# A decoder block on one Trainium2 core: the relative-position bias scratch written through a 128-partition copy, and 64 bytes of padding ahead of the weight buffers

## The chip, the core and the metric

The kernel runs on one core of a Trainium2 chip. The metric is device time in microseconds (us) of one execution. A profile is one further execution, recorded by the hardware profiler. PE is TensorE's matmul, PEld its weight load, DVE is VectorE, ACT ScalarE, POOL GpSimd, SP SyncE, which here issues the weight transfers.

## The reference

One layer for 256 tokens of width 2048, all in float32. Only what matters here is shown:

```
x = x + 0.5 * swiglu(rms_norm(x, g1), w1_gate, w1_up, w1_down)          # d_ff = 5632
z = rms_norm(x, gm) @ w_in                    # q, k, v, glu_a, glu_b, gate_a, gate_c
bias = rel_bias_table[t5_bucket(max(qpos - kpos, 0))]                   # 8 heads, 32 buckets
s = q @ k.T / 8 + bias, and -1e30 where kpos > qpos                     # two softmaxes per head
o = (softmax(s1) - lam * softmax(s2)) @ v
u = conv31(glu_a * sigmoid(glu_b)); layer norm; silu
x = x + (sigmoid(gate_a) * (o @ w_attn) + sigmoid(gate_c) * (u @ w_conv)) @ w_out
x = x + 0.5 * swiglu(rms_norm(x, g2), w2_gate, w2_up, w2_down)
out = rms_norm(x, final_g)
```

The bias depends on qpos - kpos alone, so each head's 256 x 256 bias is made of one row of 384 values, shifted by one place for each query.

## The kernel before, in words

**The matmuls.** Every product is float32 made of float32r parts. `Weights` (lines 42 to 102) streams all weights in units of 1 MB: four k-tiles by 512 columns, 8 KB in each of 128 partitions. SP issues one transfer for each unit (line 58) into one of three raw buffers `w`. `split_to` (line 76) takes half a unit at a time: ACT copies the rounded high part into `wh` (line 87), DVE subtracts to get the low part `wl` (line 88). There are four `wh` and four `wl` buffers of 4 KB per partition. A raw buffer's next transfer is issued once both of its halves are split.

Two helpers multiply. `lin` (line 292) holds a weight slice of 128 columns as the stationary operand and moves the activations: for each k-tile a "high" matmul over 512 columns (`wh`; line 305) and a "low" one over 256 columns (`wl`; line 310). One such pair is the step of all up, gate, q, k, GLU and output products, and of the first FFN's down product: 4288 pairs in all. `lin_tok` (line 341, through `tok_products`, lines 333 to 339) holds activations as the stationary operand and moves 512 columns of `wl` (line 337) or `wh` (lines 338 and 339): v, the two gates, the attention and convolution branches, and the second FFN's down product. In its very last stage (lines 880 to 894 and 902 to 915) four halves of the weights are split into `qh` and `ql`, which lie in the activations' region Q, in place of `wh` and `wl`.

**Side work.** `Side` (line 110) interleaves small jobs with the matmuls. `tick` is called once for a k-tile pair and column tile; a job of rate 0.1 takes one step in ten ticks, some 7 us of matmuls. The order of every engine's queue is thus fixed when the program is built, and an instruction on POOL that waits for nothing runs as soon as those ahead of it on POOL are done.

**The bias.** `bias_rows` (line 463) is such a job. POOL fills `bias_row` (8 partitions, one for each head, 384 values), then issues one DMA for each head (line 477) that reads that head's single partition 128 times and writes 128 rows of 384 values into the DRAM scratch `row_d` (rows 385 values apart). `bias_load` (line 652) later reads `row_d` with a row step of 384, which shifts each query's row by one. Between the job's steps POOL's queue has the gate products `s_t` of `ffn_up` (line 369), each of which waits for ACT.

**Where the tiles lie.** Tiles are laid out one after another in each partition. `xT`, the regions P and Q (two tiles of 16 KB each: activations as `h`, `a`, `hm`, `mg`, and `qh`, `ql`) and `s_t`/`y_sb` begin at multiples of 1 KB. `u_sb` (line 517) comes next, 8 x 286 values, that is 9152 bytes, or 8 x 1024 + 960. All that follows begins 960 bytes past a multiple of 1 KB: the two `sga`/`sgc` tiles of 16 KB, the three `w`, the four `wh`, the four `wl` and most work tiles.

Of the kernel before, what the change touches and what calls it, by code (L numbers as in the profile page):

```python
# [9 lines left out]
F32 = mybir.dt.float32  # L10
# [5 lines left out]
P = 128  # L16
T = 256
D = 2048
FF = 5632
H = 8  # L20
# [11 lines left out]
def bucket(n):  # L32
    if n < 16:
        return n
    return min(31, 16 + int(math.log(n / 16) / math.log(8) * 16))
# [98 lines left out]
def block_kernel(  # L134
# [5 lines left out]
    nc = tc.nc  # L140

    const = ctx.enter_context(tc.tile_pool(name="const", bufs=1))
    big = ctx.enter_context(tc.tile_pool(name="big", bufs=1))
# [3 lines left out]
    dram = ctx.enter_context(tc.tile_pool(name="dram", bufs=1, space=bass.MemoryType.DRAM))  # L147
# [310 lines left out]

    row_d = dram.tile([H, P, 385], F32, name="row_d")

    def bias_rows():
        row = work.tile([H, 384], F32, name="bias_row", tag="s2", bufs=1)

        nc.gpsimd.memset(row[:, 256:384], NEG)
        rel = 0
        while rel < 256:
            end = rel
            while end < 256 and bucket(end) == bucket(rel):  # L470
                end += 1
            b = bucket(rel)
            nc.gpsimd.tensor_copy(row[:, 256 - end:256 - rel], loads["tab"][:, b:b + 1].broadcast_to([H, end - rel]))
            rel = end
            yield
        for h in range(H):
            nc.gpsimd.dma_start(out=row_d[h:h + 1, :, 0:384], in_=row[h:h + 1].unsqueeze(1).broadcast_to([1, P, 384]))
            yield


    side.add(bias_rows(), 0.1, delay=256)


# [30 lines left out]

    neglam = small.tile([P, 1], F32, name="neglam", bufs=1)
    U0 = KW - 1
    u_sb = big.tile([P, 8, U0 + T], F32, name="u_sb")
    y_sb = big.tile([P, 8, T], F32, name="y_sb", tag="y")

    def mixer_setup():  # L520
# [462 lines left out]
```

## Time and profile before

| | |
|---|---|
| median of 3 runs | 2148.82 us (2148.69 to 2148.85) |
| profiled execution, its own time | 2143.47 us |
| its span, first to last instruction | 2141.7 us |
| mean granted TensorE clock over the span | 0.994 of 2.4 GHz |
| moved by DMA | 395.95 MB, of it 390.10 MB by the queue of SP |

The span is split into engines' busy time in the rows below. A window row gives, for a stretch, each engine's busy time and in brackets how many instructions were running in it, the granted clock as a share of 2.4 GHz, the mean busy share of the 16 DMA engines and what they moved. A timeline row is an instruction's start, its duration, engine, line and operands, and in square brackets the idle time of the engine just before it with what ended that. Matmuls overlap, so the step from one start to the next, not the duration, is what a matmul costs.

### The profile page before, as it was taken

Reading aid. Unit: us, or ns where it says so; the run is one execution under the profiler, and the core shown is the slowest. Engines: PE = TensorE matmul, PEld = TensorE weight load, DVE = VectorE, ACT = ScalarE, POOL = GpSimd, SP = SyncE. Lnnn points to the kernel's source line nnn. Section 1 sums busy time; section 2 is a strip of 40 time slices with the busy share of each in tenths; the row PEclk is TensorE's granted clock in tenths of the full one; section 3 lists DMA queues with packets and bytes.
Section 4 is the critical chain, followed back from the end, with each engine's and each line's share of the span. In section 5 each row is a group of like instructions: output and inputs, shape, how many; then the busy total and the mean of one; then the engine's idle time right before and its main releaser. Section 6 shows DMA issues by size and latency. Waiting matters only on the chain. (4 is left out here: it accounts for less than half of the span.)

```text
span 2141.7 us, 28362 instructions
## 1 busy us (share of the span) xinstructions
PE 2104.0 (98%) x11230; PEld 1790.3 (84%) x11230; DVE 1389.4 (65%) x1915; ACT 1027.7 (48%) x1456; POOL 189.0 (9%) x226
## 2 busy tenths in 40 slices
PE   8999999979999999999999999999999999999998
PEld 6888888867888888888778788888888888888887
DVE  8666556635556776789888766665654656545665
ACT  5544344433345555455555744554543444434444
POOL 6101011110011110000000000200100001000011
PEclk9999999989999999999999999999999999999999
DMA  6655555786555555555554555555555555555553
GB/s 236 203 196 180 194 186 189 192 115 214 183 192 179 186 190 197 181 180 178 182 168 169 190 183 177 177 201 192 178 197 180 180 194 193 180 193 177 197 183 132
DMA packets 57446, 395.95 MB, mean 185 GB/s; under 512 B 6864, under 2 KB 6896, under 8 KB 10464
## 3 DMA queue, kind: packets, MB, share of 16 engines
q1 hardware_dynamic: 55872, 390.10, 52.3%
q0 software_dynamic: 1440, 4.03, 2.6%
q8 instruction: 88, 1.44, 0.3%
q14 instruction: 46, 0.38, 0.0%
HBM read 390.43 MB, written 3.67 MB: 184 GB/s over the span
## 5 line engine op out<-in xcount | busy, mean ns | idle before, releaser
L88 DVE TENSOR_TENSOR wl<-w,wh 128x1024 fp32r<-128x1024 f32 x731 | 902.7, 1248 | 607.8 <-ACT wh L87 600.6
L87 ACT ACTIVATE wh<-w 128x1024 fp32r<-128x1024 f32 x731 | 764.8, 1057 | 821.2 <-PE ps_mm L305 546.5
L305 PE MATMUL ps_mm<-h,wh 128*128 128x512 f32 x2816 | 981.7, 396 | 5.9 <-DVE h L229 5.7
L310 PE MATMUL ps_mm<-h,wl 128*128 128x256 f32 x2816 | 762.4, 281 | 3.5 <-DVE wl L88 3.3
L305 PEld LDWEIGHTS ps_mm<-h,wh 128*128 128x128 f32 x2816 | 518.7, 188 | 115.0 <-ACT wh L71 5.7
L310 PEld LDWEIGHTS ps_mm<-h,wl 128*128 128x128 f32 x2816 | 528.1, 188 | 22.3 <-DVE wl L88 5.7
L305 PE MATMUL ps_mm<-a,wh 128*128 128x512 f32 x704 | 246.0, 397 | 18.1 <-ACT wh L87 18.1
L369 POOL TENSOR_TENSOR s_t<-s_t,rstd 128x256 f32<-128x256 f32 x88 | 85.7, 974 | 1201.2 <-ACT s_t L368 1201.2
L310 PE MATMUL ps_mm<-a,wl 128*128 128x256 f32 x704 | 190.9, 282 | 0.5 <-DVE wl L88 0.5
L305 PE MATMUL ps_mm<-hm,wh 128*128 128x512 f32 x512 | 178.9, 396 | 0.0
L305 PEld LDWEIGHTS ps_mm<-a,wh 128*128 128x128 f32 x704 | 130.2, 189 | 45.5 <-ACT wh L87 18.4
L310 PE MATMUL ps_mm<-hm,wl 128*128 128x256 f32 x512 | 138.4, 281 | 0.0
L310 PEld LDWEIGHTS ps_mm<-a,wl 128*128 128x128 f32 x704 | 133.0, 189 | 5.5 <-DVE wl L88 1.0
L337 PE MATMUL ps_mm<-wl,a 128*128 128x512 f32 (+1 forms) x344 | 133.9, 389 | 0.0
L338 PE MATMUL ps_mm<-wh,a 128*128 128x512 f32 (+1 forms) x344 | 133.8, 389 | 0.0
L339 PE MATMUL ps_mm<-wh,a 128*128 128x512 f32 (+1 forms) x344 | 133.8, 389 | 0.0
L337 PE MATMUL ps_mm<-wl,hm 128*128 128x512 f32 x320 | 130.6, 408 | 0.0
L339 PE MATMUL ps_mm<-wh,hm 128*128 128x512 f32 x320 | 126.5, 395 | 0.0
L338 PE MATMUL ps_mm<-wh,hm 128*128 128x512 f32 x320 | 126.4, 395 | 0.0
L305 PEld LDWEIGHTS ps_mm<-hm,wh 128*128 128x128 f32 x512 | 94.4, 188 | 20.4 <-issue 0.7
L571 DVE SCALAR_TENSOR_TENSOR y_sb<-u_sb,cw_sb,y_sb 128x256 f32<-128x256 f32 x240 | 105.3, 478 | 0.0
L354 ACT ACTIVATE rh<-ps_mm 128x256 f32<-128x256 f32 x208 | 77.5, 373 | 45.8 <-PE ps_mm L305 45.7
(192 smaller groups left out, 1808.9 us busy)
## 6 DMA issues: line engine op xcount, KB each, us to landing
w<-in_ffn_w_up_dram SPq DMA_DIRECT2D x88, 1024.0 KB, 4.9
w<-in_ffn_w_down_dram SPq DMA_DIRECT2D x88, 1024.0 KB, 4.8
w<-in_ffn_w_gate_dram SPq DMA_DIRECT2D x85, 1024.0 KB, 4.9
w<-in_w_in_dram SPq DMA_DIRECT2D x72, 1024.0 KB, 4.8
w<-in_w_out_dram SPq DMA_DIRECT2D x16, 1024.0 KB, 4.9
w<-in_w_attn_branch_dram SPq DMA_DIRECT2D x8, 1024.0 KB, 4.8
w<-in_w_conv_branch_dram SPq DMA_DIRECT2D x8, 1024.0 KB, 4.8
w<-in_ffn_w_gate_dram SPq DMA_DIRECT2D x5, 512.0 KB, 8.9
```

The lines of the kernel that those rows point to most:

```text
L87: self.nc.scalar.activation(wh, w, AF.Copy)
L88: self.nc.vector.tensor_tensor(wl, w, wh.bitcast(F32), ALU.subtract)
L305: nc.tensor.matmul(ps[ct], lhsT=w, rhs=xs(kt), start=(kt == 0), stop=(kt == nk - 1))
L310: nc.tensor.matmul(ps[ct][:, T:2 * T], lhsT=w, rhs=xs(kt)[:, 0:T], start=False, stop=False)
L337: nc.tensor.matmul(ps, lhsT=hi, rhs=wl[:, kk, :], start=(first and kk == 0), stop=False)
L338: nc.tensor.matmul(ps, lhsT=hi, rhs=wh[:, kk, :], start=False, stop=False)
L339: nc.tensor.matmul(ps, lhsT=lo, rhs=wh[:, kk, :], start=False, stop=(last and kk == KH - 1))
L354: nc.scalar.activation(r, ps[:, T:2 * T], AF.Copy, scale=scale)
L369: nc.gpsimd.tensor_tensor(s, s, rstd, ALU.mult)
L571: nc.vector.scalar_tensor_tensor(y, src, w, y, ALU.mult, ALU.add)
```

## The change

Two parts. The first replaces the eight DMAs of `bias_rows` by nine: POOL stores `row` once to a DRAM scratch `row_1` (12 KB); four DMAs, two heads each, read it back, the same 3 KB for each of 128 partitions, into a tile `spread` of 12 KB per partition in the region `sga`; four DMAs, two heads each, write `spread` to `row_d`. The scratch `row_d` gets the same values at the same places. The job has one step more. The second part makes `u_sb` 16 values longer, with the same view of it as before, so that all tiles behind it move up by 64 bytes and begin at a multiple of 1 KB.

```
+    row_1 = dram.tile([H, 384], F32, name="row_1")
     row_d = dram.tile([H, P, 385], F32, name="row_d")
 
     def bias_rows():
...
-        for h in range(H):
-            nc.gpsimd.dma_start(out=row_d[h:h + 1, :, 0:384], in_=row[h:h + 1].unsqueeze(1).broadcast_to([1, P, 384]))
+        nc.gpsimd.dma_start(out=row_1, in_=row)
+        yield
+        spread = big.tile([P, H, 384], F32, name="spread", tag="sga")
+        for h in range(0, H, 2):
+            nc.gpsimd.dma_start(out=spread[:, h:h + 2], in_=bass.AP(tensor=row_1.tensor, offset=row_1.offset + h * 384,
+                                                                  ap=[[0, P], [1, 2 * 384]]))
+            yield
+        for h in range(0, H, 2):
+            nc.gpsimd.dma_start(out=row_d[h:h + 2, :, 0:384].rearrange("h p c -> p h c"), in_=spread[:, h:h + 2])
             yield
...
-    u_sb = big.tile([P, 8, U0 + T], F32, name="u_sb")
+
+    u_sb = big.tile([P, 8 * (U0 + T) + 16], F32, name="u_sb")
+    u_sb = u_sb[:, 0:8 * (U0 + T)].rearrange("p (c t) -> p c t", c=8)
     y_sb = big.tile([P, 8, T], F32, name="y_sb", tag="y")
```

## Rows read from the trace of the kernel before

**Rows 1.** The page's first part: busy time, share of span, instructions.

```profile
PE 2104.0 (98%) x11230; PEld 1790.3 (84%) x11230; DVE 1389.4 (65%) x1915; ACT 1027.7 (48%) x1456; POOL 189.0 (9%) x226
```

**Rows 2.** Windows of 20 us; the first line names the columns.

```profile
core 0: us, PE busy (x) PEld busy (x) DVE busy (x) ACT busy (x) POOL busy (x), PEclk, DMA share, GB/s
...
460.00:480.00 20.00, 7.63 (x44) 6.42 (x42) 3.22 (x8) 1.61 (x5) 0.00 (x0) 0.76 0.93 68
480.00:500.00 20.00, 13.82 (x66) 11.67 (x67) 8.98 (x9) 7.73 (x9) 0.00 (x0) 0.73 0.73 264
...
980.00:1000.00 20.00, 20.00 (x98) 15.90 (x97) 19.41 (x41) 11.96 (x26) 0.00 (x0) 1.00 0.54 181
```

**Rows 3.** Timeline of PE around its one long gap.

```profile
467.35 0.28 PE L310 MATMUL ps_mm<-a,wl 128*128 128x256 f32 x1
485.71 0.79 PE L305 MATMUL ps_mm<-a,wh 128*128 128x512 f32 x1 [18.08 <-ACT wh L87]
...
495.15 0.39 PE L305 MATMUL ps_mm<-a,wh 128*128 128x512 f32 x1
```

**Rows 4.** Waits: engine and line, waited for, us in total, times, longest.

```profile
ACT wh L87 <- DMA w<-in_ffn_w_down_dram: 25.3, 4, 20.9
```

**Rows 5.** Timeline of POOL, its DMA issues and the instruction after them.

```profile
403.30 1.09 POOL L477 DMA_DIRECT2D row_d<-bias_row  x2 [0.30 <-POOL bias_row L473]
...
439.90 0.55 POOL L477 DMA_DIRECT2D row_d<-bias_row  x1
...
444.95 2.60 POOL L477 DMA_DIRECT2D row_d<-bias_row  x5
593.83 0.74 POOL L369 TENSOR_TENSOR s_t<-s_t,rstd 128x256 f32<-128x256 f32 x1 [146.28 <-ACT s_t L368]
```

**Rows 6.** The tile bias_row: issue to landing of its eight DMAs.

```profile
DMA to landing us min/median/max: 9.6/17.2/36.2
```

**Rows 7.** A window of 4 us while those DMAs are in flight.

```profile
456.00:460.00 4.00, 4.00 (x25) 3.46 (x23) 1.98 (x3) 1.90 (x4) 0.00 (x0) 1.00 0.95 27
```

**Rows 8.** Timeline of PE in the last stage, moving operand wl/wh, then ql/qh.

```profile
2104.80 0.39 PE L339 MATMUL ps_mm<-wh,a 128*128 128x512 f32 x1
...
2111.10 0.39 PE L339 MATMUL ps_mm<-wh,a 128*128 128x512 f32 x1
...
2112.72 0.39 PE L337 MATMUL ps_mm<-ql,a 128*128 128x512 f32 x1
...
2116.57 0.39 PE L339 MATMUL ps_mm<-qh,a 128*128 128x512 f32 x1
```

**Rows 9.** Groups of PE by form, line 337: 512-column matmuls on wl.

```profile
L337 PE MATMUL ps_mm<-wl,hm 128*128 128x512 f32 x320 | 130.6, 408 | 0.0
...
L337 PE MATMUL ps_mm<-wl,a 128*128 128x512 f32 x328 | 129.4, 395 | 0.0
...
L337 PE MATMUL ps_mm<-wl,cT 128*128 128x512 f32 x64 | 25.8, 403 | 0.0
L337 PE MATMUL ps_mm<-wl,oT 128*128 128x512 f32 x64 | 25.3, 396 | 0.0
```

**Rows 10.** Timeline of PE in lin, first and last of two runs of pairs.

```profile
105.10 0.39 PE L305 MATMUL ps_mm<-h,wh 128*128 128x512 f32 x1
...
107.89 0.39 PE L305 MATMUL ps_mm<-h,wh 128*128 128x512 f32 x1
...
599.93 0.39 PE L305 MATMUL ps_mm<-h,wh 128*128 128x512 f32 x1
...
607.70 0.40 PE L305 MATMUL ps_mm<-h,wh 128*128 128x512 f32 x1
```

**Rows 11.** DMA issues: count, KB each, median us to landing.

```profile
out_dram<-x SPq DMA_DIRECT2D x8, 256.0 KB, 2.7
...
row_d<-bias_row POOLq DMA_DIRECT2D x8, 192.0 KB, 17.2
...
fg<-in_final_norm_g_dram POOLq DMA_DIRECT2D x1, 1024.0 KB, 6.8
```

## The prediction

> **What bounds the kernel now.** I began with the page's first part: PE is busy 98% of the span, DVE 65%, ACT 48% [rows 1]. So TensorE sets the time nearly everywhere, and only two things can change it: a stretch in which PE stands still, or what one matmul costs.
>
> Windows of 20 us show PE at 20.00 in nearly every one from 40 to 2120 us; the two far below it lie together, from 460 to 500 [rows 2]. There PE works 7.63 and 13.82 us, the granted clock falls to 0.76 and 0.73 on average, and the DMA engines are 0.93 busy while they move only 68 GB/s. Another window, from 980, has a share of 0.54 and 181 GB/s. The reader should see an engine set that is occupied without moving bytes.
>
> The timeline puts the gap between 467.35 and 485.71 us: PE idles 18.08 us for ACT's split of `wh` [rows 3], and ACT had itself waited 20.9 us for a transfer of down weights [rows 4]. POOL's timeline gives the reason: two bias DMAs went out at 403.30, one at 439.90 and five back to back from 444.95, because nothing else stood in POOL's queue [rows 5]. The slowest landed 36.2 us after its issue [rows 6]. Five DMAs of 196,608 bytes in 36.2 us are 27.2 GB/s; a window amid them shows 27 GB/s for all queues together at a share of 0.95 [rows 7]. All 16 engines hold packets of the one source partition, and SP's weights sit behind them until PE's stock is used up.
>
> The cost of one matmul is read where nothing else disturbs it, in the last stage. On `wh`/`wl`, 27 steps run from 2104.80 to 2111.10: 233.3 ns each. On `qh`/`ql`, 17 steps run from 2112.72 to 2116.57: 226.5 ns [rows 8]. Line, shape and stationary tile are the same, PE never waits; only the place of the moving operand differs, 960 bytes past a multiple of 1 KB against 0.
>
> **The change, part by part.** *The stall.* From 467.35 to 495.15 PE started 39 matmuls, 19 pairs and one low, in 27.80 us [rows 3]. At the rate before the stall, 8 pairs in 2.79 us, or 348.8 ns each [rows 10], they need 19 x 0.349 + 0.12 = 6.75 us (the low taken as a third of a pair). The stall thus costs **21.05 us**: the 18.1 us gap, and some 3 us in which PE, after standing still, ran at the lower of its two levels, 1.2 GHz (the first high matmul lasts 0.79 us, the last one quoted 0.39), until the clock rose again.
>
> Is it gone? The nine new DMAs keep POOL's places: `row_1` and the first read-back near 403, the second at 440, then two read-backs and four writes from 445 on. POOL now waits for landings: the first read-back for `row_1`, each write for its read-back. Behind these waits stands only the next `s_t`, at 593.83, which now follows 146.28 us of idleness [rows 5]; nobody waits for POOL before that. The ninth issue costs another 0.5 us there (2.60 us for five). The read-back's nearest row is `fg`, the same 8 KB to 128 partitions, 1 MB in 6.8 us; so 384 KB take at most about that. The write's nearest row is `out`, 256 KB from 128 partitions in 2.7 us, so 384 KB take 4.1 us; the other end is the old DMA's 27.2 GB/s, 14.5 us [rows 6, 11]. I take 4.1, since source layout and not DRAM is what `out` and the new write share. The 36.2 us hold made a gap of 18.1 us, so PE's stock covers 18 us. The burst is 2 x 0.39 + 4 x 0.39 = 2.36 MB; at the 264 GB/s of the recovering window [rows 2] that is 9 us. It fits twice, so I count the whole 21.05 us. If the cover fails, weights are late again at the same place.
>
> *The pad.* It moves all behind `u_sb` from 960 to 0 modulo 1024. The moving operands on line 337 outside region Q are 320 + 328 + 64 + 64 = 776 matmuls of 512 columns [rows 9], and lines 338 and 339 have as many: 2328. At 233.3 - 226.5 = 6.8 ns each that is **15.8 us**. Ends: 0, if something other than alignment separates the two places, and 15.8. I take 15.8, because the pair of rows differs in little else. The one stage where a faster PE may meet another engine is around 980 to 1000, DVE at 19.41 of 20 us [rows 2]; it is short, and I leave its tenths of a us to the range.
>
> [...]
>
> *lin.* Its 512- and 256-column moving operands lie in P and Q, already at multiples of 1 KB; only the stationary slices move. Its pairs run at two rates, 348.8 ns and, 22 pairs from 599.93 to 607.70, 353.2 ns [rows 10], on the same code and the same buffers. So I take **0**. The ends: were each half of a pair to gain as the rows of the last stage do (2.9%), 10 ns on 4288 pairs, 44 us. The other way, all pairs at one of the two rates against all at the other differ by 4288 x 4.4 ns = 19 us; a program laid out anew may fall either way, so 8 us up or down for the range.
>
> *Costed at nothing:* the ACT and DVE splits and the weight transfers start at other addresses, but PE hides them (DVE 65%, ACT 48%); `spread` takes `sga`, whose next user is written only in the mixer; one further step of the job delays nothing that is due.
>
> **Sum.** 2143.47 - 21.05 - 15.8 = 2106.6 for the profiled execution, which stands 5.35 us (0.25%) below the median of the runs. Against the median: 2148.82 - 36.85 = **2112.0 us**.
>
> **Rivals.** (a) *The pad does nothing.* For it: the two places differ in address as well as alignment, and lin's two rates show that steps can differ for other reasons. Against: inside the last stage the rate changes exactly with the operand. 2148.82 - 21.05 = **2127.8**. [...]
>
> (b) *lin gains as well*, by its stationary slices: 2112 - 44 = **2068**. For: lin's high matmul has an aligned moving operand and still does not step at 226.5. Against: its two rates at equal addresses, which alignment cannot explain.
>
> (c) *The slow side was the DRAM write*, rows of 1536 bytes at a step of 1540, not the single source partition. Then the last burst grows from 5 x 0.197 to 4 x 0.393 = 1.57 MB, at 27.2 GB/s 57.8 us; the hold is 21.6 us longer and so is the gap. With the pad's gain 2148.82 + 21.6 - 15.8 = **2154.6**, slower. It decides once the burst holds the weights over 52 us, where what the stall gains in length outweighs the pad. For: the rows are the same as before. Against: `out` writes at 97 GB/s including its latency [rows 11].
>
> (d) *A remnant of the stall*: four writes of 4.1 us in a row and two reads make 19 us or more, just past the cover. A gap of a few us and a spell at the lower clock: 2116 to 2124.
>
> **How the numbers follow.** Forecast 0.55, (a) 0.22, (b) 0.12, (c) 0.05, (d) 0.06. The time is the forecast's. The range goes from 2097 (the forecast with lin at its quicker rate, and part of (b)'s gain) to 2133 (rival (a), with some of lin's loss); it leaves out most of (b) and all of (c). A measurement of this kernel tells about 0.2% (4 us) from no change. All cases but (c) lie more than that below 2148.8; I keep 0.03 of them back for mishaps that cancel. So faster 0.92, same 0.03, slower 0.05.
>
> **What would show it.** Right: no gap of PE near 467, windows 460 to 500 at 20.00 with the clock at 1.00; read-backs and writes of 384 KB landing within 10 us; steps of 226 to 227 ns on lines 337 to 339 throughout, also on `wl` and `wh` in the last stage, equal to those on `ql`. Wrong on the pad: 233 ns stays there. Wrong on lin: pairs near 340 ns. Wrong on the write: landings over 14 us and ACT again waiting for down weights. DVE ending waits of PE between 960 and 1200 would mean that the pad's gain was spent there.

## The result and the profile after

The changed kernel takes 2117.49 us, median of 4 runs (2115.86 to 2119.97), against 2148.84 us of the kernel before in the same comparison (4 runs, 2148.69 to 2149.89). The ratio is 0.9854, interval 0.9837 to 0.9871: faster by 31.3 us. The forecast was 2112.0 us, 36.8 us faster. The profiled execution took 2117.11 us, its span is 2115.3 us (2141.7 before) and its mean granted clock 0.999.

The first part of the page after, which answers to [rows 1]:

```profile
PE 2095.2 (99%) x11230; PEld 1788.2 (85%) x11230; DVE 1390.4 (66%) x1915; ACT 1027.4 (49%) x1456; POOL 190.7 (9%) x227
```

The instructions are the same but for one more on POOL. PE is still the bound, and its busy time has fallen by only 9 us: most of the 26 us of span was idle time. The windows of after that answer to [rows 2], with the one ahead of them:

```profile
core 0: us, PE busy (x) PEld busy (x) DVE busy (x) ACT busy (x) POOL busy (x), PEclk, DMA share, GB/s
440.00:460.00 20.00, 20.00 (x114) 17.34 (x113) 12.46 (x16) 9.84 (x15) 8.31 (x11) 1.00 0.69 236
460.00:480.00 20.00, 20.00 (x115) 17.36 (x114) 13.19 (x20) 9.85 (x15) 0.00 (x0) 1.00 0.71 271
480.00:500.00 20.00, 20.00 (x115) 17.32 (x115) 11.82 (x16) 7.30 (x7) 0.00 (x0) 1.00 0.52 175
```

Before, 44 and 66 matmuls ran in the last two of these; now it is 115 each, at a granted clock of 1.00. The first of the three was this before:

```profile
440.00:460.00 20.00, 20.00 (x117) 17.46 (x115) 12.12 (x13) 9.98 (x14) 5.40 (x8) 1.00 0.98 90
```

From 440 to 480 us the DMA engines were 0.98 and then 0.93 occupied for 90 and 68 GB/s; now they are 0.69 and 0.71 occupied and move 236 and 271 GB/s. The timeline of POOL after, its DMA issues, which answers to [rows 5]:

```profile
407.51 0.54 POOL L477 DMA_DIRECT2D row<-bias_row  x1 [0.29 <-POOL bias_row L474]
412.55 0.58 POOL L481 DMA_DIRECT2D spread<-row  x1 [4.50 <-DMA row<-bias_row]
...
449.66 1.11 POOL L481 DMA_DIRECT2D spread<-row  x2
450.76 1.46 POOL L485 DMA_DIRECT2D row_d<-spread  x2
456.79 0.71 POOL L485 DMA_DIRECT2D row_d<-spread  x1 [4.57 <-DMA spread<-row]
458.04 0.72 POOL L485 DMA_DIRECT2D row_d<-spread  x1 [0.54 <-DMA spread<-row]
```

The new waits are there, as costed: 4.50 us for `row_1`, 4.57 and 0.54 us for read-backs, and nothing of POOL's is due before 578. What the long wait [rows 4] became stands in the list of waits after; the line under it is the landing of all DMAs that touch the tile `spread`, read-backs and writes together:

```profile
ACT wh L87 <- DMA w<-in_ffn_w_down_dram: 2.4, 1, 2.4
```

```profile
DMA to landing us min/median/max: 3.6/8.5/11.9
```

ACT's longest wait for down weights fell from 20.9 to 2.4 us and none of PE's waits comes from it any more. No transfer of the bias takes over 11.9 us, where one took 36.2 [rows 6].

The timeline of PE after in the last stage, moving operand `wl`/`wh` and then `ql`/`qh`, answering to [rows 8], and two rows of `lin` that answer to [rows 10]:

```profile
2075.74 0.39 PE L338 MATMUL ps_mm<-wh,a 128*128 128x512 f32 x1
...
2084.80 0.39 PE L339 MATMUL ps_mm<-wh,a 128*128 128x512 f32 x1
2085.03 0.39 PE L337 MATMUL ps_mm<-ql,a 128*128 128x512 f32 x1
...
2090.24 0.39 PE L339 MATMUL ps_mm<-qh,a 128*128 128x512 f32 x1
```

```profile
602.88 0.40 PE L305 MATMUL ps_mm<-h,wh 128*128 128x512 f32 x1
...
611.71 0.40 PE L305 MATMUL ps_mm<-h,wh 128*128 128x512 f32 x1
```

On `wl`/`wh` 40 steps take 9.06 us, 226.5 ns each, and on `ql`/`qh` 23 steps take 5.21 us, also 226.5: the 233.3 ns of before have gone. In `lin`, 25 pairs take 8.83 us, 353.2 ns each. That is the slower of its two rates before, and it is now by far the commoner: in every stretch of 60 us in which `lin` works, from 60 to 720 us and after 1500, the mean pair takes 353.2 to 353.5 ns, but for 1860 (352.9). It isn't the only one. Outside those stretches `lin` at times runs quicker, as here:

```profile
1441.23 0.39 PE L305 MATMUL ps_mm<-h,wh 128*128 128x512 f32 x1
...
1455.10 0.39 PE L305 MATMUL ps_mm<-h,wh 128*128 128x512 f32 x1
```

These are 40 pairs, 346.8 ns each, on buffers at the same places. So two rates remain, and each holds for dozens of pairs.

For the whole kernel I take the mean of all steps from one matmul's start to the next, steps under 260 ns only, so that waits stay out: some 4240 of the 4288 512-column steps of `lin` (line 305), 4285 of its 256-column steps (line 310), and 2312 of the 512-column steps of `lin_tok` (lines 337 to 339; 48 of them on `qh`/`ql`, the others on `wl`/`wh`). Before: 232.1 + 119.6 = 351.7 ns a pair, and 233.2 ns in `lin_tok`. After: 235.8 + 117.4 = 353.2 ns, and 227.4 ns. So `lin` lost 1.56 ns x 4288 = 6.7 us and `lin_tok` won 5.8 ns x 2312 = 13.4 us.

### The profile page after: what moved, and what is told of

It is laid out like the page before. It is cut to its first block, busy times and chain, and to the rows that moved or that the text cites. A ratio compares the mean times of both kernels' runs of the same rounds, so it can differ in the third digit from the quotient of the medians.

```text
span 2115.3 us, 28367 instructions
## 1 busy us (share of the span) xinstructions
PE 2095.2 (99%) x11230; PEld 1788.2 (85%) x11230; DVE 1390.4 (66%) x1915; ACT 1027.4 (49%) x1456; POOL 190.7 (9%) x227
```

## The experiments

Places below are the remainder of a tile's address modulo 1 KB, worked out from the order and sizes of the tiles. "Weights" are `w`, `wh`, `wl` and the tiles behind them; P and Q hold the activations. (With the new bias part `spread` is the first tile to take the region `sga`, which then lies ahead of `u_sb`, pad or no pad; the places of `wh` and `wl` don't change by it.) Before, the weights lie at 960 and P and Q at 0; after, all lie at 0. All diffs are against the kernel after unless it says otherwise. The kernel before ran beside each group: 2147.39 us (8 runs) for the first four, 2145.15 (1 run) for the next four, 2146.57 (9 runs) for the last four.

**Each part alone.** The first kernel has the bias part and no pad:

```
-    u_sb = big.tile([P, 8 * (U0 + T) + 16], F32, name="u_sb")
-    u_sb = u_sb[:, 0:8 * (U0 + T)].rearrange("p (c t) -> p c t", c=8)
+    u_sb = big.tile([P, 8, U0 + T], F32, name="u_sb")
```

> The first part of the change alone (bias scratch through 128 partitions; no pad, weight buffers stay at 960 modulo 1024). Theory T (three terms: the stall is worth 21 us, the pad speeds lin_tok's steps and slows lin's pairs): the gap near 467 is gone, lin_tok steps stay at 233.2 ns, lin's pairs stay a mixture of 348.9 and 353.2 ns with a mean of about 351.7, time 2148.8 - 21 = 2128 us. Rival R (lin's slower rate in the changed kernel comes from the missing stall or the different timing, not from the pad): lin's pairs are at 353.3 throughout here too, 1.6 ns more on 4288 pairs, time about 2134.5 us.

Measured: 2123.01 us (4 runs, 2121.58 to 2126.42), ratio 0.9893, interval 0.9876 to 0.9910. Its windows:

```profile
460.00:480.00 20.00, 20.00 (x115) 17.45 (x114) 12.96 (x19) 9.89 (x16) 0.00 (x0) 1.00 0.68 263
480.00:500.00 20.00, 20.00 (x115) 17.40 (x114) 11.61 (x15) 7.53 (x8) 0.00 (x0) 1.00 0.58 199
```

The stall is gone by this part alone. Four rows of PE, two stretches of `lin`:

```profile
601.70 0.40 PE L305 MATMUL ps_mm<-h,wh 128*128 128x512 f32 x1
...
611.96 0.39 PE L305 MATMUL ps_mm<-h,wh 128*128 128x512 f32 x1
...
806.29 0.39 PE L305 MATMUL ps_mm<-hm,wh 128*128 128x512 f32 x1
...
821.99 0.39 PE L305 MATMUL ps_mm<-hm,wh 128*128 128x512 f32 x1
```

The first two are 29 pairs apart, 353.8 ns each; the last two 45 pairs, 348.9 ns each. So with the weights at 960 both rates are still there, in one program and between the same buffers of weights, but over another mixture than before (mean pair 352.6 ns against 351.7). All matmuls, their order and the places of their operands are the same in this kernel and in the one before, and yet from 60 to 420 us, ahead of the old stall, the mean pair takes 349.8 ns before and 353.1 here. The place alone thus doesn't set which rate `lin` runs at; what does is open. `lin_tok` stays at 233.2 ns. The expectation's theory T had the mean pair at 351.7 and the rival at 353.3; 352.6 lies between them, and the time is 5 us below the 2128 of theory T.

The second kernel has the pad and the old eight bias DMAs (against the kernel before):

```
-    u_sb = big.tile([P, 8, U0 + T], F32, name="u_sb")
+    u_sb = big.tile([P, 8 * (U0 + T) + 16], F32, name="u_sb")
+    u_sb = u_sb[:, 0:8 * (U0 + T)].rearrange("p (c t) -> p c t", c=8)
```

> The pad alone, the eight old bias DMAs kept. Theory T: the gap near 467 is there as before (about 18 us of PE idle and a spell at the lower clock), lin_tok steps fall from 233.2 to 226.7 ns (about 13 us, a little less than 2328 x 6.5 because the attention stage has other steps between), lin's pairs are 353.3 ns throughout (6.7 us lost), time 2148.8 - 13.3 + 6.7 = 2142 us. Rival R: lin's pairs keep the mixture of before, time about 2135.5 us.

Measured: 2140.0 us (5 runs, 2137.75 to 2140.31), ratio 0.9964, interval 0.9951 to 0.9978. One of its windows, and the row of its list of waits that holds PE's gap:

```profile
460.00:480.00 20.00, 12.79 (x73) 10.82 (x71) 6.11 (x12) 3.52 (x8) 0.00 (x0) 0.87 0.96 37
```

```profile
PE ps_mm L305 <- ACT wh L87: 19.1, 1, 19.1
```

The gap is whole, and so the pad is worth 0.36%, some 7.7 us, by itself; theory T's 2142 us was 2 us too long. The two ratios multiply to 0.9857; the whole change has 0.9854. The parts add up. With the pad `lin_tok` is at 227.4 ns and the mean pair of `lin` at 353.5 (353.2 without the stall); without the pad it was 351.7 and 352.6. In these four profiles the pad so costs `lin` 0.7 to 1.9 ns a pair, 3 to 8 us: the mixture at 960 moves by itself, and the size of the loss moves with it.

**The order of `lin`'s matmuls.** A pair alternates 512 and 256 columns. One theory was that this switch of size costs the extra nanoseconds. All low products of a column tile are put together, and all high ones:

```
+            n = len(pair) * KH
...
-                for i in range(len(pair) * KH):
-                    if pair[0] * KH + i < nk - 1:
-                        high(ct, i)
-                        low(ct, i)
-                    else:
-                        low(ct, i)
-                        high(ct, i)
+                low_first = len(pair) > 1 or (pair[0] > 0 and ct % 2 == 1)
+                for part in ((low, high) if low_first else (high, low)):
+                    for i in range(n):
+                        part(ct, i)
```

> The changed kernel with another order of the matmuls in lin: for a column tile all high matmuls (512 columns), then all low ones (256 columns), and for the next column tile the other way round, so that PE goes from one size to the other once or less for two pairs, not twice for each pair. Theory S (a pair costs 353 and not 340 ns because PE changes between the two sizes): the extra 13 ns fall to 3 to 7 ns, a pair costs 343 to 347 ns, 26 to 43 us less: 2075 to 2092 us. Rival (the extra is paid by each matmul for the place of its operands): pairs stay near 353, time 2117 us; slower by some us if PE now waits for the low parts in bursts.

Measured: 2107.34 us (4 runs, 2106.78 to 2107.50), ratio 0.9817, interval 0.9800 to 0.9834, so some 10 us below the kernel after. The mean high and low steps add up to 350.8 ns, 2.5 less than after, where theory S wanted 6 to 10 and its rival none. Order matters a little, and the size switch isn't most of it.

**Other places of the weights.** A pad of 32 bytes puts them at 992 (`+ 16]` becomes `+ 8]` in `u_sb`), one of 96 bytes at 32 (`+ 24]`):

> The changed kernel with a pad of 32 bytes in place of 64: the weight buffers begin 992 bytes past a multiple of 1 KB. Theory A (only a start at a multiple of 1 KB, or of a smaller power of two above 32, makes the 512-column read cheap): lin_tok steps are 233.2 ns as at 960, lin's pairs as in the kernel before, time 2127 to 2128 us. Rival B (what counts is some other property of the place, which a shift of 32 bytes would also change): lin_tok steps at 226.7 ns, or at a third value.

> The changed kernel with a pad of 96 bytes: weight buffers 32 bytes past a multiple of 1 KB. Theory A (lin_tok's 512-column read is cheap at a multiple of 1 KB only): lin_tok steps 233.2 ns. For lin two ways: like 960 (a mixture of 348.9 and 353.2; time about 2127 us) if only the 64-byte remainder counts in some other way, or like 992 (347.5; time about 2107 us) if half a line of 64 bytes is what helps lin.

Measured, one run each: 2107.40 us at 992 and 2130.48 us at 32. At 992 `lin` steps faster than anywhere before; the first and last of 44 pairs:

```profile
595.83 0.39 PE L305 MATMUL ps_mm<-h,wh 128*128 128x512 f32 x1
...
611.09 0.39 PE L305 MATMUL ps_mm<-h,wh 128*128 128x512 f32 x1
```

That is 346.8 ns a pair here, 347.7 over the kernel, and the slow rate of 353 doesn't occur; but `lin_tok` is back at 233.1 ns. At 32 neither gains: 353.3 and 233.2 ns. (The line of 64 bytes in the expectation was the author's guess; no run shows one.) So both helpers depend on the place of the weights, each in its own way, and a multiple of 1 KB is the best of the four places for `lin_tok` (227.4 ns against 233.1 to 233.2) and, with 32, the worst for `lin` (353.2 and 353.3 ns against 347.7 and 352.6).

**`wh` and `wl` apart.** With a tile of 32 bytes between them one lies at 992 and the other at 0. First `wh` at 992, `wl` at 0:

```
+        self.pool.tile([P, 8], F32, name="gap", tag="gap", bufs=1)
...
-    u_sb = big.tile([P, 8 * (U0 + T) + 16], F32, name="u_sb")
+    u_sb = big.tile([P, 8 * (U0 + T) + 8], F32, name="u_sb")
```

> The changed kernel with wh at 992 and wl at 0 modulo 1024. lin_tok: a third of its steps (line 337) at 226.7 ns, two thirds at 233, 4.4 us less than with all at 992. Theory H (lin's rate hangs on where the high part wh lies, the stationary operand of the 512-column matmul): pairs at 347.7 ns, time about 2103 us. Theory L (it hangs on wl): pairs at 353.2, time about 2127 us.

Then the mirror image, with `wl` allocated first, then the gap, then `wh`:

> The mirror image: wl at 992, wh at 0 modulo 1024. lin_tok: two thirds of its steps at 226.7 ns, 8.9 us less than with all at 992. Theory H: pairs at 353.2 ns, time about 2122 us. Theory L: pairs at 347.7 ns, time about 2098.5 us. If both places count, pairs near 350 here and in the mirror image.

Measured, one run each: 2095.88 us and 2128.02 us. Both times lie outside what was expected. `lin` goes the way of theory H, quick with `wh` at 992 and slow with `wh` at 0, but `wl` counts too. With `wh` at 992 and `wl` at 0 a pair takes 345.4 ns, less than with both at 992 (347.7) or both at 0 (353.2); its 512-column step falls from 235.8 to 226.9 ns. The mirror image gives 352.7. `lin_tok` keeps little of its gain in either (231.3 on `wl` and 233.8 on `wh`; 234.0 and 231.7). So the place of one operand alone doesn't decide a step, nor does that of a matmul's own two operands. With `wl` and the activations both at 0, as after, the step on `wl` takes 231.3 ns here and 227.4 after; with `wh` at 992 and the activations at 0, the 512-column step of `lin` takes 226.9 ns with `wl` at 0 and 229.4 with `wl` at 992. Of what the matmuls read, only the neighbours' operand lies elsewhere in each couple.

Order and place together, the grouped order with the weights at 992:

> lin's matmuls grouped by size as in the earlier run, with all weight buffers at 992. If order and place act on separate parts of a pair's extra time: 347.7 - 2.5 = 345 ns, time about 2097 us. If they act on the same part: 347.7, about 2107 us.

Measured, one run: 2117.10 us, 350.3 ns a pair. Neither expectation holds. Grouping makes `lin` quicker at 0 (353.2 to 350.8) and slower at 992 (347.7 to 350.3), so the two don't add, and the theory of the size switch is not what explains the pairs.

**Is it the address, or how the operands lie to each other?** A tile of 32 bytes ahead of P and Q moves them and all behind them. First everything at 32, so that the operands lie to each other as after:

```
+    big.tile([P, 8], F32, name="gap_pq")
```

> Everything 32 bytes further: the activations' regions P and Q and the weight buffers all at 32 modulo 1024, so that they lie to each other as in the changed kernel. Theory Rel (a matmul's step hangs on how its two operands lie to each other): lin_tok at 227.4 ns and lin's pairs at 353.2 as in the changed kernel, time about 2117 us. Theory Abs (it hangs on where the moving operand itself begins): lin_tok at 233 ns as with weights at 32 before, lin's pairs 353 or more, since now their 512-column moving operand is off its multiple too; time 2130 us or more.

Then P and Q at 32 with the weights at 0 (that line, and `+ 8]` in `u_sb`), to each other as weights at 992 and P, Q at 0:

> P and Q at 32, weight buffers at 0 modulo 1024: to each other as in the run with all weights at 992. Theory Rel: lin_tok 233 ns, pairs 347.5 ns, time about 2107 us. Theory Abs: lin_tok at 227 ns (its moving operand, the weights, lies at 0), lin's 512-column step up by some 6 ns, time 2117 to 2145 us.

And P, Q and `wl` at 32 with `wh` at 0 (both lines, and the gap between `wh` and `wl`), to each other as in the best kernel so far:

> P and Q at 32, wh at 0, wl at 32 modulo 1024: to each other as in the run with wh at 992 and wl at 0. Theory Rel: pairs 345.4 ns, time about 2096 us. Theory Abs: the low and the high matmul's moving operand both begin at 32, pairs above 350 ns, time 2110 us or more.

Beside them the best one was timed again, over five runs:

> The kernel of the run with wh at 992 and wl at 0 once more, timed. It gave 2095.9 us in one look, 345.4 ns for a pair. If that is its steady state and not one draw: 2094 to 2099 us, about 1% below the changed kernel's 2117.5 and 2.4% below the kernel before.

Rows of PE in `lin`, first and last of a run of pairs, in the order of these four kernels, all at 32 first:

```profile
603.04 0.40 PE L307 MATMUL ps_mm<-h,wh 128*128 128x512 f32 x1
...
611.87 0.40 PE L307 MATMUL ps_mm<-h,wh 128*128 128x512 f32 x1
```

```profile
595.92 0.39 PE L307 MATMUL ps_mm<-h,wh 128*128 128x512 f32 x1
...
610.48 0.39 PE L307 MATMUL ps_mm<-h,wh 128*128 128x512 f32 x1
```

```profile
595.64 0.39 PE L308 MATMUL ps_mm<-h,wh 128*128 128x512 f32 x1
...
605.98 0.39 PE L308 MATMUL ps_mm<-h,wh 128*128 128x512 f32 x1
```

```profile
595.90 0.39 PE L306 MATMUL ps_mm<-h,wh 128*128 128x512 f32 x1
...
604.86 0.39 PE L306 MATMUL ps_mm<-h,wh 128*128 128x512 f32 x1
```

They are 25, 42, 30 and 26 pairs: 353.2, 346.7, 344.7 and 344.6 ns each. Everything shifted by 32 bytes steps like the kernel after, P and Q shifted alone step like the weights at 992, and the third steps like its counterpart, the fourth. The times follow: 2117.91 us against 2117.49; 2106.81 against 2107.40; 2095.40 against 2095.88. Each couple agrees within 0.03%, one run each against the earlier time, though P, Q, `wh` and `wl` all moved by 32 bytes. So for this shift the theory that the absolute remainder decides has fallen; what counts is how P and Q, `wh` and `wl` lie to each other. The best kernel took 2096.12 us (5 runs, 2094.09 to 2096.60), ratio 0.9765, interval 0.9751 to 0.9778: 21 us below the kernel after.

All kernels without the stall in one table; the pair and the `lin_tok` step are the means described above. The last two columns compare with the kernel after: (pair - 353.2) x 4288 + (step - 227.4) x 2312, with unrounded means, and the span less 2115.3 us.

| weights / P, Q | us | pair, ns | `lin_tok`, ns | by steps, us | span, us |
|---|---|---|---|---|---|
| 0 / 0 (after) | 2117.49 | 353.2 | 227.4 | 0 | 0 |
| 960 / 0 (bias part alone) | 2123.01 | 352.6 | 233.2 | +10.5 | +9.4 |
| 0 / 0, grouped | 2107.34 | 350.8 | 227.4 | -10.5 | -9.8 |
| 992 / 0 | 2107.40 | 347.7 | 233.1 | -10.3 | -9.7 |
| 32 / 0 | 2130.48 | 353.3 | 233.2 | +13.8 | +13.4 |
| `wh` 992, `wl` 0 / 0 | 2096.12 | 345.1 | 233.0 | -22.1 | -23.0 |
| `wl` 992, `wh` 0 / 0 | 2128.02 | 352.7 | 232.5 | +9.6 | +10.9 |
| 992 / 0, grouped | 2117.10 | 350.3 | 233.2 | +0.5 | 0.0 |
| 32 / 32 | 2117.91 | 353.5 | 227.5 | +1.4 | +0.8 |
| 0 / 32 | 2106.81 | 347.8 | 233.1 | -10.1 | -10.3 |
| `wh` 0, `wl` 32 / 32 | 2095.40 | 345.2 | 233.0 | -21.3 | -21.7 |

The mean steps of the two helpers account for every span within 1.5 us, so whatever else differs between these kernels adds up to no more: PE is the bound in all of them.

## Why the prediction was right, and where a term was off

**The stall** was read rightly. The bias part alone takes the gap of PE away, and with the old DMAs and the pad it is there, 19.1 us long. Its size in the profiled executions: the bias part alone has a span 17.0 us shorter than before, and its pairs cost 0.9 ns x 4288 = 3.9 us more, so the stall was 20.9 us, against 21.05 in the sum. The single source partition was the slow side, not the rows of `row_d`: the same rows of 1536 bytes written from 128 partitions landed in 11.9 us at most. The four writes, 1.57 MB, were issued from 450.76 to 458.04 and so had landed by 469.9, which is 82 GB/s or more; the last five of the old ones, 0.98 MB, took 38.3 us from the first issue, at 444.95, to the last landing, or 25.7 GB/s. (The 27.2 GB/s of the prediction counted the five over the 36.2 us of the slowest one alone, which is short by the 2 us in which they were issued.) Rival (c) fell with that, and (d) with the windows, in which PE no longer stands still. That SP's weights sat behind the bias shows in the trace of before: from 456 to 460 us POOL's queue took 94.6% of the time of the 16 engines and SP's queue moved nothing, and the four weight transfers issued between 440 and 480 landed after a median of 32.4 us, where over the whole kernel it is 4.8. The spell at the lower clock is there too, as a share: the granted clock is 1.00 up to 470, falls while PE stands, is 0.50 from 471 to 490, and 1.00 from 491 on. At 0.50 four pairs from 487.99 to 490.55 take 0.64 us each. The trace gives no clock in GHz. The 768 columns of a pair in 0.64 us are 1.2 a ns at a share of 0.50, which makes 2.4 at 1.00: 1.2 and 2.4 GHz stand as an estimate from these pairs, at a column a cycle.

**The landings** were longer than costed: the read-backs' median is 6.3 us, within the bound of 6.8, but the writes' median is 9.6 us, between the 4.1 that I took from `out` and the 14.5 at the other end, and one took 11.9, over the 10 us that I named as a sign of being right. Their small rows or the weights beside them may be why; the runs don't separate these. It cost nothing that shows: the engines kept moving SP's weights meanwhile (236 and 271 GB/s in all), and PE had no gap.

**The pad in `lin_tok`** had the right sign and rate, 233.3 to 226.5 ns in the last stage, as rows said. Over all its matmuls the mean gain is 5.8 ns, from 233.2 to 227.4, and so 13.4 us instead of 15.8. Rival (a) fell. DVE ends one wait of PE between 960 and 1200 us, 0.9 us long, so the gain was not spent there.

**The step that failed is the term "lin: 0".** I argued that only stationary slices move and that two rates at equal addresses are something which alignment cannot explain, and put the difference between the rates into the range alone. With the pad `lin` runs nearly always at the slower of the two: 353.2 ns a pair against a mean of 351.7, a loss of 6.7 us that gives back half of the pad's gain. The ends of that term held it (8 us). Where the stationary operands lie does count, by up to 8 ns a pair (353.2 to 345.1), but a placement doesn't fix one rate: at 960 pairs of 349 and of 353 ns occur, in shares that differ between two kernels without a change of place; at 0 most take 353.3 and some 346.8. So the thought that something other than the place is at work was right, and it was no reason for 0. What sends `lin` into one rate or the other no run shows, and that it mostly found the slower one here was not foreseen. Rival (b), pairs near 340 ns, fell for this change, though its thought that the stationary slices matter was nearer to the truth than my term.

**The sum** by measured terms is -20.9 - 13.4 + 6.7 = -27.6 us, against -26.4 by the two spans. Profile against profile, 10 us of the forecast's 36.85 are missing; by the medians only 5.5. The medians differ by 31.3 us, 5 more than the spans, because the profiled execution of before stands 5.35 us under its median, as the prediction had it, while that of after stands at its own. That the forecast came so close is luck to that extent. What makes executions of the kernel before differ by up to 7 us (2143.06 to 2150.12) wasn't taken apart; its mixture of `lin`'s rates is a candidate, but only one program was profiled twice, the one with `wh` at 992 and `wl` at 0: 345.4 and 345.1 ns a pair, 1.2 us of the 1.8 us between its two spans.

**The mechanism** was stated too simply. "A multiple of 1 KB" isn't what helps: with everything at 32 the kernel is as quick (2117.91 against 2117.49 us), and with `wh` 32 bytes short of the multiple it is 21 us quicker. The runs show that it matters here how the operands of neighbouring matmuls lie to each other (345.1 to 353.5 ns a pair in one order of the matmuls), and that beside this PE held two rates at one placement (353.2 and 346.8 ns with all at 0). What in that relation makes the nanoseconds is not shown. Nor were other differences tried, nor a layout that gives each helper its best place at once: by the means above, 345.1 ns pairs with 227.4 ns steps would take (233.0 - 227.4) x 2312, an estimated 13 us, off the best kernel, if such a layout exists.

## What to carry to other kernels

Where the DMA engines show a high busy share and few GB/s (here 0.98 and 90), look for a queue whose source lies in one partition; a trip through DRAM that spreads it over 128 partitions can cost less than what it frees for the others (here 25.7 GB/s became 82 or more, and the stall of 20.9 us went). Where PE is the bound and matmuls of one shape step at different rates (here 233.3 and 226.5 ns), treat the placement of their operands to each other, neighbouring matmuls included, as a parameter, and measure each helper's step by itself, since what is best for one may cost another (the pad: 13.4 us won in `lin_tok`, 6.7 us lost in `lin`). A rate that a change leaves alone in the code may not stay if one of its operands moves (here from 351.7 to 353.2 ns a pair): the term belongs into the sum at its nearest rate, with a sign, not at nothing.

## What the runs showed of the hardware that was not expected

A shift of 32 bytes between the operands changed a matmul's step: the 512-column step of `lin` was 235.8 ns with `wh`, `wl` and activations at equal places and 226.9 ns with `wh` alone 32 bytes lower. One step went against the other in the same kernel: with the pad `lin`'s 512-column step rose by 3.7 ns (232.1 to 235.8) while its 256-column step fell by 2.2 (119.6 to 117.4). And the same code with its weights in the same buffers held 353.8 and 348.9 ns a pair in one execution (353.2 and 346.8 with the pad), each over dozens of pairs, with the granted clock at 1.00 around all four stretches. At the slow rate the steps repeat every three pairs: with the pad the 512-column ones take about 233, 241 and 236 ns in turn, with everything at 32 they take 230, 240 and 230 by starts given to 0.01 us; at 346.8 ns all of them take 230.
